# A decoder block on one core: all five engines in an order that the kernel's own clocks set, and a delta-rule chain cut differently

## The chip, the cores and the metric

The kernel runs on one core of one Trainium2 chip. The time is the device time of one execution in microseconds (us). Before: 3033.8 us, the median of three runs (3033.46 to 3036.6).

The core has several engines that run side by side, each with its own queue that it takes in order: TensorE (PE, matrix products, into PSUM), VectorE (DVE), ScalarE (ACT), GpSimd (POOL) and SyncE (SP), which in this kernel issues the DMA transfers. An engine waits where its next instruction needs a result of another engine or of a transfer that isn't there yet.

## The reference

One decoder block over 2048 tokens of width 1024, batch 1, all in 32-bit floats:

```python
mod = einsum(silu(c), ada_w) + ada_b;  shift, scale, gate = split(mod, 3)
h = rmsnorm(x, norm_g) * (1 + scale) + shift
p = h @ w_in                                   # 1024 -> 9344 columns
c_val, c_gate, c_og, ts, r_og, g_conv, g_rwkv = split(p)
y_conv = conv_branch(c_val, c_gate, c_og)      # GLU, depthwise conv of width 31, LayerNorm, swish, SiLU gate, @ w_conv_out
y_rwkv = rwkv7_branch(ts, r_og)                # 16 heads of 64
m = sigmoid(g_conv) * y_conv + sigmoid(g_rwkv) * y_rwkv
x = x + gate * (m @ w_out)
return rmsnorm(x, final_g)
```

The RWKV branch mixes each token's `ts` with that of the token before (token shift), forms r, k, v, a decay w and a rate a per channel, and carries a 64x64 state per head over the tokens:

```python
sk = state @ kk_t
state = state * w_t - sk (x) b_t + v_t (x) k_t
o_t = state @ r_t
```

Then follow a LayerNorm per head, the bonus term sum(r k r_k) v, a SiLU gate and a projection with `w_rwkv_out`.

## The kernel before, in words

**Blocks and groups.** The 2048 tokens are cut into 4 blocks of 512 (b), the 16 heads into 4 groups of 4 (g), and a group into two pairs of heads (q), one pair per 128 partitions. So there are 16 slots (b, g), one after the other in `slot` (L1039), and the state of a group goes on from block to block. All arrays stand with channels on the partitions and 512 tokens along the row.

**Projections.** The columns of `w_in` are 73 tiles of 128. For each tile and block, `project` (L849) makes a 128x512 result in one PSUM bank from 24 matmuls (`mm3k`, L172 to L180; the matmul is L179): eight steps of 128 input channels, and for each the products hi·hi, hi·lo and lo·hi of weights and input that were split into a coarse and a fine part. The weights are split in block 0 (`load_w`, L149 to L170: ACT makes hi, POOL or DVE makes lo), written to DRAM (kh_in, kl_in) and read back in blocks 1 to 3. The input of a block is split by `hprep` (L409) from `hload` (L401). Each slot has 18 projections: k, r and v for its two pairs, two channel tiles of the convolution branch with two projections each, and eight gates. Their filler order is in `FILL` (L46).

**Stages between the projections.** Everything else on PE stands between projection matmuls. A cooperative scheduler (`Task`, `poll`, `tick`, `drain`, L223 to L265) runs while the program is traced: a stage is a piece of a generator that ends in `yield pe, delay`, two constants, the estimated PE time of the stage and a delay until the next one may be placed; `mm3` adds 0.684 us per step of a projection to the clock and polls. On PE the traced order is the order on the chip (`tc.manual_schedule(engines={PE})`, L1084). The order on DVE, ACT, POOL and SP is chosen by the framework's own scheduler, with priorities (`HP`, `LOWP`).

**A pair** (`pair`, L501 to L630): the decay's pre-activation (L513 to L516), its running sum within each chunk of 64 tokens (eight scans of 64 columns on DVE, L522 to L524), its exponentials, the arrays KR and BK (k, r and b scaled by the decay, L544 to L570), the norms of kk (L551), the 128x128 products within each chunk (`As`, L587 with the mask at L590), their strict triangle scaled (`tri`, L597), transposes of BK (`tk`, L607), the bonus (L613), and the values transposed into `uv` (L623).

**A group** (`group`, L645 to L847) takes its two pairs' tiles and goes through these steps:
- The inversion. The 32x32 diagonal blocks of the triangles go to DRAM by 16 small transfers (dA, L657), come back with one block per partition (La, L662), and POOL inverts them in 31 steps of two instructions (L669 to L674). The results go back by way of DRAM (dT, L677, and 16 transfers into As, L684). Two fixed delays of 35 and 25 us stand behind this (L686, L688), and the next stage waits until the group before is done.
- The correction. DVE transposes the blocks (T11, L705); two stages of small matmuls (`lower` L718, `upper` L722, with Qs at L728) make the off-diagonal blocks; no other stage may come between (`locked`).
- The chain: for each of the 8 chunks c, three stages on PE with work on DVE and ACT between them. KR stage (L775): KR times the state S, on 128x128 tiles; DVE adds Xz (L780) and ACT scales the state (Se, L779). Middle stage (L784): the inverse times Xz by head, with the next chunk's `xval` (L749) and the outputs of the chunk before, `olast` (L758), which ACT copies (L762); DVE scales the result into uv (L795). State stage (L800): tk times uv, two matmuls with 128 columns, of which the diagonal 64x64 blocks are used; DVE adds them to Se (S, L804).
- The end: LayerNorm per head (L822 to L831) on DVE, ACT and POOL, a fixed delay of 30 us (L832), transposes back into one PSUM bank `late` (L839), scaling (oc, L841), bonus and gate from DRAM on POOL (L845), and the result to DRAM.

**Beside these**: the convolution (`taps`, L872 to L890: 31 multiply-adds of 128x512 on DVE per channel tile, at low priority), the token shift (`shifted`, L465 to L474, whose first column, L472, and carry, L474, are on DVE), the LayerNorm of the convolution branch of the block before (`lnorm_first`), the norm of the next block's input (`xnorm`), and the splitting of the later weights (`presplit`, L131).

**The second phase** (from L1090): the projections with `w_rwkv_out`, `w_conv_out` and `w_out`, the residual and the final norm.

Of the kernel before, what the change touches and what calls it, by code (L numbers as in the profile page):

```python
# [33 lines left out]
W2 = 4  # L34
# [12 lines left out]
US_MM, US_K = 0.228, 0.684  # L47
LOWP = 1500
# [18 lines left out]
def hybrid_block(ctx: ExitStack, tc: tile.TileContext, x, vecs, convk, w2a2, final_g, ada, w_in, w_co, w_ro, w_o, crow, out,  # L67
                 seq=2048, groups=(0, 1, 2, 3), phase2=True, dbg=None):
    nc = tc.nc
    NB = seq // TB  # L70
    dbg = dbg or {}
# [20 lines left out]
    make_identity(nc, ident)  # L92
# [11 lines left out]

    def rsqrt(y, x_, pool, eng, t=None):
        if t is None:
            t = pool.tile(list(x_.shape), F32, name="rs_t", tag="rs_t")
        eng.tensor_scalar(out=y.bitcast(I32), in0=x_.bitcast(I32), scalar1=-0.5, scalar2=float(0x5F3759DF),
                          op0=ALU.mult, op1=ALU.add)
        for _ in range(3):  # L110
            eng.tensor_tensor(out=t, in0=y, in1=y, op=ALU.mult)
            eng.scalar_tensor_tensor(out=t, in0=t, scalar=-0.5, in1=x_, op0=ALU.mult, op1=ALU.mult)
            eng.scalar_tensor_tensor(out=y, in0=t, scalar=1.5, in1=y, op0=ALU.add, op1=ALU.mult)
# [9 lines left out]
    lo_dve = [False]  # L123
# [7 lines left out]
    def presplit(name, n, half):  # L131

        i = f"{n[0]}_{n[1]}" if name == "o" else n
        back = kept.setdefault((name, n), [dp.tile([P, KT, P], F32R, name=f"k{p_}_{name}{i}", tag=f"k{p_}_{name}{i}")
                                           for p_ in "hl"])
        hs = slice(half * 4, half * 4 + 4)
        st, hi, lo = hx("w_st"), hx("w_hi"), hx("w_lo")
        nc.sync.dma_start(st.rearrange("p (k n) -> p k n", k=4), wsrc[name][n][:, hs, :])
        if name == "o":
            gr = hx("w_gr")  # L140
            nc.sync.dma_start(gr[:, :256], grow_d[n[0] * 256:n[0] * 256 + 256].unsqueeze(0).broadcast_to([P, 256]))
            s4 = st.rearrange("p (k n) -> p k n", n=256)
            nc.gpsimd.tensor_tensor(out=s4, in0=s4, in1=gr[:, :256].unsqueeze(1).broadcast_to([P, 2, 256]), op=ALU.mult)
        nc.scalar.copy(hi.bitcast(F32R), st)
        nc.gpsimd.tensor_tensor(out=lo.bitcast(F32R), in0=st, in1=hi, op=ALU.subtract)
        for d_, s_ in zip(back, (hi, lo)):
            nc.sync.dma_start(d_[:, hs, :].bitcast(F32), s_.rearrange("p (k n) -> p k n", k=4))

    def load_w(name, n, hl=None):  # L149
# [11 lines left out]
        with tc.high_priority(HP):  # L161
            nc.scalar.copy(hi, st)  # L162
            lo_eng = nc.vector if lo_dve[0] or (name != "in" and wcount[0] % 4 < W2) else nc.gpsimd
# [17 lines left out]

    def mm3(ps, w, a):
        for k in range(KT):
            mm3k(ps, w, a, k)
            tick(US_K)
# [35 lines left out]
    now, tasks = [0.0], []  # L221

    class Task:  # L223

        def __init__(self, gen):
            self.gen, self.at, self.cond, self.done = gen, now[0], None, False
            tasks.append(self)

        def ready(self):
            return self.at <= now[0] and (self.cond is None or self.cond())  # L230

        def step(self):
            try:
                r = next(self.gen)
            except StopIteration:
                self.done = True
                tasks.remove(self)
                return
            if callable(r):
                self.cond = r  # L240
            else:
                self.cond = None
                now[0] += r[0]
                self.at = now[0] + r[1]

    def poll():
        moved = True
        while moved:
            moved = False
            for t in list(tasks):  # L250
                if not t.done and t.ready():
                    t.step()
                    moved = True

    def tick(us):
        now[0] += us
        poll()

    def drain(*ts):
        poll()  # L260
        while not all(t.done for t in ts):
            at = [t.at for t in tasks if t.at > now[0] and (t.cond is None or t.cond())]
            assert at, "no task can go on"
            now[0] = min(at)
            poll()  # L265

# [26 lines left out]
    bf = lt.tile([P, P], F32, name="bf", tag="X", bufs=1)  # L293
# [13 lines left out]
    one = c1.tile([P, CH], F32, name="one")  # L307
    nc.vector.memset(one, 1.0)
    maskA = c1.tile([P, 4, CH], F32, name="maskA")
    m64 = lt.tile([64, 2, CH], F32, name="m64", tag="X", bufs=1)  # L310
# [35 lines left out]
    closed = [None]  # L346

    def hx(name):
        return xp.tile([P, TB], F32, name=name, tag="hx")

    def spare(name):
        return closed[0](name) if closed[0] else hx(name)

    def xnorm(b, tts):
        if not tts:
            return
        held = []
        for tt in tts:
            t0 = b * TB + tt * P
            ss = e2.tile([P, 8], F32, name="ss")  # L360
            xh = []
            for half in range(2):
                xt = hx("xt")
                nc.sync.dma_start(xt, x[t0:t0 + P, half * TB:half * TB + TB])
                xh.append(xt)
            for half in range(2):
                nc.scalar.activation(hx("xsq"), xh[half], AF.Square, accum_out=ss[:, half:half + 1])
            vs, rs = ss[:, 2:3], ss[:, 3:4]
            with tc.high_priority(HP):
                nc.vector.tensor_tensor(out=vs, in0=ss[:, 0:1], in1=ss[:, 1:2], op=ALU.add)  # L370
# [668 lines left out]
    def slot(b, g, h, lora, first):  # L1039
        drain(*side, *groups_[-2:-1])  # L1040
        G = opened(b, g, h, lora)
        if first:
            G.wait = 8.0
# [274 lines left out]
```

## Time and profile before

| what | value |
|---|---|
| runs | 3036.6, 3033.8, 3033.46 us |
| median | 3033.8 us |
| the profiled execution | 3034.01 us |
| its span | 3032.2 us |
| granted clock of TensorE, mean | 0.969 |
| DMA | 680.00 MB, 224 GB/s over the span |

The span goes from the first to the last record of the profile; the time of the execution is a little longer. The page gives busy time per engine, groups of instructions by line with the idle time ahead of them and what ended it, and the DMA issues. PE is matrix products, PEld weight loads (they overlap PE), SPq the queue on which SyncE issues transfers; `x` is a count, `tile<-tile` names what is written and what is read, and in a row of the timeline the first two columns are start and duration in us. A record of PE is not always an instruction: a matmul of 32-bit floats leaves two records.

### The profile page before, as it was taken

The page shows a single profiled execution, that of the slowest core. Times are in us where ns is not written, and L with a number is a line of the kernel's source. Part 1 is how long each engine was busy: PE and PEld are TensorE (multiplying, and loading weights), DVE is VectorE, ACT ScalarE, POOL GpSimd, SP SyncE. Part 2 cuts the span into 40 slices and gives each one's busy share as a digit, 9 for nine tenths or more (in the row PEclk, how much of TensorE's full clock was granted, in tenths as well). Part 3 has the DMA queues.
Part 4 walks back from the last instruction along what each step waited for, and adds up shares of the span by engine and source line. Part 5 has one row for each costly group of instructions (what it writes and reads, how often), then busy time and mean ns, then how long its engine had stood idle before and what let it go on. Part 6 is the DMA issues. An engine that isn't in the chain of part 4 may idle for free. (4 is left out here: it accounts for less than half of the span.)

```text
span 3032.2 us, 51026 instructions
## 1 busy us (share of the span) xinstructions
PE 2817.1 (93%) x18640; PEld 2297.6 (76%) x18640; DVE 2072.0 (68%) x4160; ACT 1001.3 (33%) x1936; POOL 1229.8 (41%) x1790
## 2 busy tenths in 40 slices
PE   6889798999799999999999999999999999899998
PEld 5767686777687777777878777778787778788988
DVE  6867777779676778676767777666778755753433
ACT  4424343434233324242423242323323323421211
POOL 3464637352536355425373655253644500400000
PEclk9989899999899999999999999999999999999999
DMA  8677657686757666857676668565656666976665
GB/s 309 234 247 249 217 204 257 204 268 197 241 187 258 198 203 218 284 173 240 191 257 203 210 217 305 168 208 171 193 184 213 237 210 195 336 250 222 215 222 174
DMA packets 363146, 680.00 MB, mean 224 GB/s; under 512 B 135632, under 2 KB 154384, under 8 KB 362896
## 3 DMA queue, kind: packets, MB, share of 16 engines
q1 hardware_dynamic: 362896, 676.75, 67.0%
q8 instruction: 147, 2.41, 0.3%
q14 instruction: 103, 0.84, 0.1%
HBM read 494.08 MB, written 181.41 MB: 223 GB/s over the span
## 5 line engine op out<-in xcount | busy, mean ns | idle before, releaser
L179 PE MATMUL ps_main<-h_hi,w_hi 128*128 128x512 f32 x2304 | 970.6, 421 | 19.7 <-DMA w_hi<-kh_in 15.1
L179 PE MATMUL ps_main<-h_hi,w_lo 128*128 128x512 f32 x2304 | 918.6, 399 | 7.2 <-POOL w_lo L164 4.0
L179 PE MATMUL ps_main<-h_lo,w_hi 128*128 128x512 f32 x2304 | 915.4, 397 | 1.3 <-DVE h_lo L397 1.1
L890 DVE SCALAR_TENSOR_TENSOR acc<-u,ck,acc 128x512 f32<-128x512 f32 x928 | 696.7, 751 | 15.9
L179 PEld LDWEIGHTS ps_main<-h_hi,w_hi 128*128 128x128 f32 x2304 | 442.9, 192 | 115.5 <-issue 9.9
L179 PEld LDWEIGHTS ps_main<-h_hi,w_lo 128*128 128x128 f32 x2304 | 440.7, 191 | 114.4 <-POOL w_lo L164 6.2
L179 PEld LDWEIGHTS ps_main<-h_lo,w_hi 128*128 128x128 f32 x2304 | 443.6, 193 | 81.6 <-DVE h_lo L397 2.9
L804 DVE SCALAR_TENSOR_TENSOR S<-xo,pe,Se 64x64 f32<-64x64 f32 x512 | 144.5, 282 | 140.1 <-PE xo L800 130.5
L671 POOL TENSOR_TENSOR itmp<-La,TT 128x126 f32<-128x126 f32 (+22 forms) x496 | 179.8, 363 | 130.2 <-DMA La<-dA 85.2
L162 ACT CAST w_hi<-w_st 128x1024 fp32r<-128x1024 f32 x103 | 108.1, 1049 | 301.4 <-DMA w_st<-w_co_t 124.8
L673 POOL TENSOR_TENSOR TT<-TT,itmp 128x126 f32<-128x126 f32 (+22 forms) x496 | 191.3, 386 | 36.8
L164 POOL TENSOR_TENSOR w_lo<-w_st,w_hi 128x1024 fp32r<-128x1024 f32 x50 | 120.4, 2408 | 131.2 <-ACT w_hi L162 67.3
L779 ACT ACTIVATE Se<-S,pe 128x128 f32<-128x128 f32 x256 | 88.9, 394 | 169.5 <-DVE S L804 169.4
L164 DVE TENSOR_TENSOR w_lo<-w_st,w_hi 128x1024 fp32r<-128x1024 f32 x53 | 65.6, 1238 | 97.2 <-PE ps_main L179 54.8
L795 DVE TENSOR_TENSOR uv<-xo,rn 64x256 f32<-64x256 f32 x128 | 53.6, 419 | 111.4 <-PE xo L784 99.3
L784 PEld LDWEIGHTS xo<-Xz,As 128*64 128x64 f32 x1024 | 70.0, 138 | 68.8 <-DVE Xz L780 32.0
L753 ACT COPY Xz<-xo 64x256 f32<-64x256 f32 x128 | 47.0, 367 | 211.9 <-PE xo L758 141.7
L780 DVE TENSOR_TENSOR Xz<-xo,Xz 64x256 f32<-64x256 f32 x128 | 53.5, 418 | 86.0 <-PE xo L775 78.9
L845 POOL TENSOR_TENSOR oc<-oc,zt 128x512 f32<-128x512 f32 x64 | 81.7, 1285 | 66.6 <-ACT oc L841 39.6
L784 PE MATMUL xo<-Xz,As 128*64 128x64 f32 x1024 | 87.9, 230 | 20.9 <-DVE Xz L780 20.8
L590 DVE TENSOR_TENSOR As<-aux,maskA 128x512 f32<-128x512 f32 x128 | 83.0, 682 | 30.9 <-PE aux L587 30.4
L587 PE MATMUL aux<-KR,BK 64*128 64x128 f32 x1024 | 82.2, 291 | 17.8 <-DVE As L590 9.3
(299 smaller groups left out, 5493.7 us busy)
## 6 DMA issues: line engine op xcount, KB each, us to landing
w_hi<-kh_in SPq DMA_DIRECT2D x219, 512.0 KB, 4.2
w_lo<-kl_in SPq DMA_DIRECT2D x219, 512.0 KB, 5.3
w_st<-w_in_t SPq DMA_DIRECT2D x73, 512.0 KB, 4.5
kh_in<-w_hi SPq DMA_DIRECT2D x71, 512.0 KB, 2.9
kl_in<-w_lo SPq DMA_DIRECT2D x71, 512.0 KB, 3.6
lny<-y_d SPq DMA_DIRECT2D x72, 256.0 KB, 4.4
w_hi<-kh_ro SPq DMA_DIRECT2D x32, 512.0 KB, 3.9
w_lo<-kl_ro SPq DMA_DIRECT2D x32, 512.0 KB, 5.3
```

The source lines that it names most:

```text
L162: nc.scalar.copy(hi, st)
L164: lo_eng.tensor_tensor(out=lo, in0=st, in1=hi.bitcast(F32), op=ALU.subtract)
L179: nc.tensor.matmul(ps[:, qs], ww[:, k, :], aa[k][:, qs], start=(k == 0 and t == 0 and q == 0), stop=(k == KT - 1 and t == 2 and q == ms - ...
L587: nc.tensor.matmul(pA[hh][:, c // 2, es], BK[hs, cc, es], KR[hs, cc, es], start=(c == 0), stop=(c == 3), skip_group_check=True)
L590: nc.vector.tensor_tensor(out=Asb[:, hh, c4 * 4:c4 * 4 + 4, :].rearrange("p (a e) n -> p a (e n)", e=2), in0=pA[hh], in1=flat(maskA).unsqu ...
L671: nc.gpsimd.tensor_tensor(out=tmp[:, :ni, :nt], in0=La[:, j:j + 1, j + 1:].broadcast_to([P, ni, nt]), in1=TT[:, :ni, j:j + 1].broadcast_to ...
L673: nc.gpsimd.tensor_tensor(out=TT[:, :ni, j + 1:], in0=TT[:, :ni, j + 1:], in1=tmp[:, :ni, :nt], op=ALU.add)
L779: nc.scalar.mul(Se[:, q, :], Sg[:, q, :], R[q]["pe"][:, c:c + 1])
L784: nc.tensor.matmul(b_[pr_, q, hs], As[q][:, hh, c, kcol(e)], Xz[:, e, q, hs], start=(n == 0), stop=(n == 3), skip_group_check=True)
L804: nc.vector.scalar_tensor_tensor(out=Sg[hs, q, hs], in0=b_[hs, 2 + q, hs], scalar=R[q]["pe"][hs, c:c + 1], in1=Se[hs, q, hs], op0=ALU.mult ...
L845: nc.gpsimd.tensor_tensor(out=oc, in0=oc, in1=zt, op=op)
L890: nc.vector.scalar_tensor_tensor(out=acc if i + 1 < HALO else yj, in0=u[:, i:i + TB], scalar=ck[:, j, i:i + 1], in1=acc, op0=ALU.mult, op1 ...
```

## The change

**All engines in traced order.** The handle `nc` is wrapped, so that every instruction is recorded as it is traced, and `manual_schedule()` now holds for all engines. `note` keeps a clock for PE (`now`), DVE, ACT, POOL, SP and the transfers (DMA), and the reckoned end of every tile; a stage yields a condition (`ok` of tiles, `bank` of a PSUM tag, `idle` of an engine, `when` something is done) and is placed when the clocks say that it holds. Constants of time within the tasks (35, 25 and 30 us among them) fall away.

```diff
+    def note(name, op, out, ins):
+        t = max([now[0], vt.get(name, 0.0), used.get(k_, 0.0)] + [ready.get(key(a), 0.0) + SEM for a in ins])
...
+        if name == "PE":
...
+                c = 0.015 + N_ / 2400 if kd == F32R else 2 * max(0.107 * M_ / 128, N_ / 1200) * (
+                    0.55 if K_ <= 64 else 0.75 if M_ <= 64 else 1.0)
+            if kd != kind[0]:
+                kind[0], c = kd, c + SWITCH
...
+        elif name == "SP":
+            vt["SP"] = t + 0.07
+            vt["DMA"] = max(vt["DMA"], t) + size(out) * out.shape[0] * 4 / DMA_RATE
+            end = vt["DMA"] + 1.9
+        else:
+            c0, c1_ = RATE[name]
+            end = vt[name] = t + c0 + c1_ * max([size(out)] + [size(a) for a in ins[:1]])
...
-    with tc.manual_schedule(engines={mybir.EngineType.PE}):
+    with tc.manual_schedule():
```

Weights come through a class `Load`, two projections ahead (three where they come back from DRAM); rings of buffers (`hx`, `t2`, `w`) give a buffer out when it is free; the steps after a projection (token shift, gates, convolution input) are tasks of their own (`evac`). The DVE taps are placed when DVE's clock is at most 0.7 us ahead. The next block's input is split within the last projection of a block (`khook`). The last slot has its own filler order (`LAST`). Block 0's projections with `w_rwkv_out` and `w_conv_out`, the first of the second phase, are traced by the tasks too while the last group ends (`early_rows`). Side work (LayerNorm of the convolution branch, `presplit`, `xnorm`) runs as one task of low rank, with `lnorm_first` in group 2 and the presplits 2, 2, 0, 4 per slot instead of 2 in each.

**The pair.** ACT adds 1, and one scan over 512 columns, with a multiplier `keep` that is 0 at the start of each chunk, takes the place of eight:

```diff
-        for c in range(NCH):
-            cs = slice(c * CH, c * CH + CH)
-            nc.vector.tensor_tensor_scan(out=M[:, cs], data0=one, data1=M[:, cs], initial=0.0, op0=ALU.add, op1=ALU.add)
...
+        nc.scalar.activation(M, M, AF.Identity, bias=one1[:, 0:1])
+        yield ok(M)
+        nc.vector.tensor_tensor_scan(out=M, data0=keep, data1=M, initial=0.0, op0=ALU.mult, op1=ALU.add)
```

In `shifted` the first column and the carry move to ACT:

```diff
+        nc.scalar.activation(dst[:, 0:1], ps[:, 0:1], AF.Identity, scale=mu1[:, mi:mi + 1], bias=carry[:, mi:mi + 1])
+        nc.scalar.activation(carry[:, mi:mi + 1], ps[:, TB - 1:TB], AF.Identity, scale=mu)
...
-        nc.vector.scalar_tensor_tensor(out=dst[:, 0:1], in0=carry[:, mi:mi + 1], scalar=mu, in1=t1[:, 0:1],
-                                       op0=ALU.mult, op1=ALU.add)
-        lastv[0] = nc.vector.tensor_copy(carry[:, mi:mi + 1], ps[:, TB - 1:TB])
```

**The inversion.** The 16 dA transfers and both La loads are issued when both pairs' triangles are reckoned to be done; each POOL step waits until POOL's clock is at most 0.5 us ahead; the As transfers go in fours; the correction waits for the chain of the group before, not for its end:

```diff
-        yield lambda: G.tri == 2
+        yield when(lambda: G.tri == 2)
+        yield ok(*As)
...
+        yield ok(La, TT)
         for j in range(31):
+            yield idle("POOL", 0.5)
...
+        yield ok(dT)
...
-        yield 0.0, 35.0
...
-        yield 0.0, 25.0
-        yield lambda: G.pairs == 2 and (before is None or before.done)
+                yield idle("SP", 0.1)
+        yield when(lambda: G.pairs == 2 and (before is None or before.chained))
+        yield ok(*As)
```

**The chain.** The outputs leave the middle stage and become a stage of their own after each odd chunk, for two chunks whose matmuls come by turns on the two halves of the array's columns; the state stage works by head, with four products of 64x64 by turns on the halves, in place of two of 128x128:

```diff
         def olast(c):
-            vr, rc = vrow(c % 2), rcol(c % 2)
             for n, (q, hh, hs) in enumerate(every):
-                nc.tensor.matmul(xo[c % 2][vr, q, hs], As[q][:, hh, c, rc], uv[:, c, q, hs],
-                                 start=False, stop=(n == 3), skip_group_check=True)
+                for e in range(2):
+                    nc.tensor.matmul(xo[e][vrow(e), q, hs], As[q][:, hh, c + e, rcol(e)], uv[:, c + e, q, hs],
+                                     start=False, stop=(n == 3), skip_group_check=True)
+            with tc.high_priority(HP):
+                for e in range(2):
+                    nc.scalar.copy(O[vrow(e), c // 2], xo[e][vrow(e), 0:2])
...
-            if c:
-                olast(c - 1)
...
-            yield 1.1, 2.5
-            for q in range(2):
-                nc.tensor.matmul(b_[:, 2 + q, :], R[q]["tk"][:, c, :], uv[:, c, q, :], start=False, stop=(q == 1),
-                                 skip_group_check=True)
+            yield ok(uv)
+            for q, hh, hs in every:
+                nc.tensor.matmul(b_[hs, 2 + q, 0:64], R[q]["tk"][:, c, hs], uv[:, c, q, hs], start=False,
+                                 stop=(q + hh == 2), skip_group_check=True)
...
-            yield 0.6, 3.3
-        olast(NCH - 1)
-        ocopy(NCH - 1)
+            yield ok(Sg)
+            if e:
+                olast(c - 1)
+                yield ok(uv)
+        G.chained = True
```

**The end of a group.** Bonus and gate are loaded ahead of the transposes, which wait for the reckoned end of the norm and for the bank instead of 30 us.

More of the change, by code (lines that the diff above doesn't have):

```diff
@@ L33 @@
 HP = 3000
-W2 = 4
+W2 = 0.3
 HB = 8
@@ new lines, in until, with drain, after, ok @@
+    def until(pred):
+        poll()
+        while not pred():
+            ws = [w for w in (t.when() for t in tasks) if w is not None and w > now[0]]
+            assert ws, "no task can go on"
+            now[0] = min(ws)
+            poll()
+    def drain(*ts):
+        until(lambda: all(t.done for t in ts))
+    def after(us):
+        at = now[0] + us
+        return lambda: at
+    def ok(*aps):
+        ks = [key(a) for a in aps]
+        return lambda: max(ready[q] for q in ks)
+    def idle(name, us):
+        return lambda: vt[name] - us
@@ L919, in lnorm_first @@
+        yield both(ok(ys), free, bank("late"))
         ps = pl.tile([P, TB], F32, name="late", tag="late")
```

856 lines of the change are left out of this document (565 added, 291 removed).

## The prediction

> **What bounds the kernel now.** I read the page first, then the busy times by stretch, then the waits of TensorE alone, and last the timeline of single stages.
>
> ```profile
> span 3032.2 us, 51026 instructions
> PE 2817.1 (93%) x18640; PEld 2297.6 (76%) x18640; DVE 2072.0 (68%) x4160; ACT 1001.3 (33%) x1936; POOL 1229.8 (41%) x1790
> ...
> 56.00:2440.00 2384.00, 2222.04 (x15052) 1782.09 (x15050) 1747.47 (x3529) 825.92 (x1581) 1166.81 (x1736) 0.97 0.67 221
> 2440.00:3032.20 592.20, 565.22 (x3467) 492.67 (x3467) 281.44 (x514) 150.13 (x312) 44.25 (x29) 0.98 0.68 229
> ```
>
> TensorE (PE) is busy 93% of the span, and no other engine comes near. In the two lines by stretch the columns are the stretch, then busy time of PE, weight loads, VectorE (DVE), ScalarE (ACT) and GpSimd (POOL), then clock and DMA. The first stretch is the part that the change rewrites; in it PE idles 2384.0 - 2222.0 = 162 us. The second is mostly code that the change leaves alone. So there are two ways to gain: fewer idle microseconds out of 162, or less PE work. What ends the idle time, in the first stretch (us in total, times, longest):
>
> ```profile
> PE late L839 <- POOL uv L831: 23.3, 4, 16.1
> PE xo L784 <- DVE Xz L780: 20.8, 14, 3.8
> PE ps_main L179 <- DMA w_hi<-kh_in: 15.1, 3, 5.8
> PE late L839 <- ACT oc L841: 14.4, 15, 1.1
> PE aux L587 <- DVE As L590: 9.3, 7, 4.5
> PE late L722 <- DVE Qs L728: 9.1, 8, 1.9
> PE late L718 <- DVE T L705: 7.9, 2, 4.6
> PE aux L587 <- POOL KR L570: 7.8, 6, 2.8
> PE xo L758 <- DVE S L804: 7.5, 3, 4.4
> ```
>
> These rows hold 115 us; the other 47 lie in rows under 6 us each. PE takes its instructions in the order in which the program is traced, so each row is a stage that was traced too early for its data.
>
> **The change, part by part: PE work.** A short stage interrupts the projection matmuls. Those follow each other at 54.70/240 = 0.228 us (row below). I price a stage as the start of the second projection matmul after it, less the start of the last one before it, less two times 0.228.
>
> ```profile
> 2651.57 54.70 PE ps_main L179 x240
> ```
> ```profile
> 546.89 0.40 PE L179 MATMUL ps_main<-h_hi,w_lo 128*128 128x512 f32 x1
> ...
> 547.73 0.63 PE L758 MATMUL xo<-uv,As 128*64 128x64 f32 x8
> ...
> 548.63 0.40 PE L179 MATMUL ps_main<-h_lo,w_hi 128*128 128x512 f32 x1
> ...
> 550.93 0.39 PE L179 MATMUL ps_main<-h_hi,w_lo 128*128 128x512 f32 x1
> 551.16 0.60 PE L800 MATMUL xo<-uv,tk 128*128 128x128 f32 x4
> ...
> 551.83 0.40 PE L179 MATMUL ps_main<-h_lo,w_hi 128*128 128x512 f32 x1
> ```
> ```profile
> 523.48 0.40 PE L179 MATMUL ps_main<-h_hi,w_lo 128*128 128x512 f32 x1
> 523.81 0.27 PE L784 MATMUL xo<-Xz,As 128*64 128x64 f32 x1
> ...
> 524.27 0.22 PE L749 MATMUL xo<-uv,As 128*64 128x64 f32 x1
> ...
> 524.77 0.40 PE L179 MATMUL ps_main<-h_lo,w_hi 128*128 128x512 f32 x1
> ```
> ```profile
> 517.30 0.40 PE L179 MATMUL ps_main<-h_hi,w_lo 128*128 128x512 f32 x1
> 517.63 0.63 PE L551 MATMUL aux<-bones,sq 128*64 128x2 f32 x16
> ...
> 518.53 0.40 PE L179 MATMUL ps_main<-h_lo,w_hi 128*128 128x512 f32 x1
> 518.77 0.40 PE L179 MATMUL ps_main<-h_hi,w_lo 128*128 128x512 f32 x1
> 519.09 0.68 PE L749 MATMUL xo<-uv,As 128*64 128x64 f32 x8
> ...
> 520.04 0.40 PE L179 MATMUL ps_main<-h_lo,w_hi 128*128 128x512 f32 x1
> ```
>
> Per chunk now: the middle stage with its outputs costs 548.63 - 546.89 - 0.456 = 1.28, the same stage in a first chunk, without outputs, 524.77 - 523.48 - 0.456 = 0.83, and the state stage 551.83 - 550.93 - 0.456 = 0.44. So outputs that ride along cost 0.45. The last fence shows why turns look good and what they cost. L749 alone, eight records (a matmul of f32 leaves two) on one half of the columns, costs 520.04 - 518.77 - 0.456 = 0.81. L551, sixteen records that alternate between the halves, within one PSUM tile, costs 518.53 - 517.30 - 0.456 = 0.77. Turns halve the time of a record. But a stage on 128x64 tiles has a fixed part: from 523.81 to 524.27 fifteen records follow at 0.031, sixteen are 0.49, and 0.83 - 0.49 = 0.34 remains. A stage on the whole array, 0.44 for four records, shows none: its second row follows its first at projection pace.
>
> After the change the outputs of two chunks (sixteen records in turns) are a stage of their own, 0.83 per two chunks, and the state stage becomes eight records in turns on 128x64: 0.83 less eight records at 0.031, 0.58 (no row has just this; not below 0.25, the records alone, nor above 0.81, L749 without overlap; I take 0.58 because L551 overlaps within one tile). Two chunks cost 2 x (1.28 + 0.44) = 3.44 before and 2 x (0.83 + 0.58) + 0.83 = 3.65 after. There are 128 chunks: 64 x 0.21 = **+13 us**, with ends 64 x 2 x (0.25 - 0.58) = -42 and 64 x 2 x (0.81 - 0.58) = +29 around that. So the part that saves matmul time pays it back in tile changes. In the built programs' order such changes of tile size number 555 before and 895 after.
>
> The Trainium skill says as much: "TensorEngine Tiling (Array Packing)", section "Key Properties", has a change of tiling mode, as against a change of tile, drain TensorE; the 0.34 above agrees. Its section "Theoretical Speedup" gives up to twice the rate for a small dimension of 64 or less: by that alone outputs and state stage would halve, 128 x (0.45 + 0.44) / 2, an estimate of 57 us gained.
>
> **Waits that go.** In the changed program a stage is placed by readiness and by a free PSUM bank, not by a constant. Between the last state stage and the final transposes (L839) its order has 63 to 144 projection matmuls, 14 to 33 us, and the second transpose waits for its bank behind more of them: of 37.7 us I keep 5, -33. Chain (20.8 + 7.5): the steps now have only 3 to 9 projection matmuls between them, 0.7 to 2.1 us, where DVE may still be inside a tap; I keep a third, -19. The correction stage (9.1 + 7.9): -14. The block boundary (15.1): the next input is now split inside the last projection; I keep 5, -10. The pair stages (17.1): kept, since their DVE and POOL work is the same. Of the 47 in small rows: -20. Together **-96**, between 0 and -150.
>
> **Moved: the inversion's round trip.** The changed program issues all sixteen small dA transfers of a group in one run on SP after the second pair's tiles; both La loads follow, and the POOL steps stand on POOL's queue from the time its clock gives.
>
> ```profile
> 2009.66 6.60 SPq L684 DMA_DIRECT2D As<-dT  x14
> ```
> ```profile
> 2095.32 1.13 SPq L662 DMA_DIRECT2D La<-dA  x2
> ```
> ```profile
> L673 POOL TENSOR_TENSOR TT<-TT,itmp 128x126 f32<-128x126 f32 (+22 forms) x496 | 191.3, 386 | 36.8
> L671 POOL TENSOR_TENSOR itmp<-La,TT 128x126 f32<-128x126 f32 (+22 forms) x496 | 179.8, 363 | 130.2 <-DMA La<-dA 85.2 <-DMA w_lo<-kl_in 9.6
> ```
> ```profile
> La<-dA SPq DMA_DIRECT2D x32, 256.0 KB, 4.5
> ...
> As<-dT SPq DMA_DIRECT2D x256, 16.0 KB, 1.9
> ...
> dT<-TT SPq DMA_DIRECT2D x32, 128.0 KB, 4.0
> ```
> ```profile
> L705 DVE STREAM_TRANSPOSE T<-As 32x128 f32<-32x128 f32 x128 | 31.0, 277 | 9.5 <-DMA As<-dT 8.2
> ```
>
> One small transfer holds SP for 6.60/14 = 0.47 us, where the new clock (SP's line in note) reckons 0.07. A group needs: sixteen issues 7.5, La 0.6 and its landing 4.5, POOL (191.3 + 179.8)/16 = 23.2, dT 0.5 + 4.0, sixteen issues back 7.5, landing 1.9, eight transposes 2.2: 52 us, plus what else POOL does in between, 3 us or more. What PE has to do meanwhile is in the order: in the last group of each block 153 to 171 projection matmuls stand between the second pair's tiles and the inversion's first matmul, 35 to 39 us, 40 to 47 with the other stages among them; in the other twelve groups 237 to 318, 54 to 73 us, 66 to 86 with the stages (before: 216 to 279 everywhere). So four groups come out short, by 11, 11, 8 and 15 us: **+45** (0 if other waits of PE cover it). While POOL stands at the first step, the next pair's KR and BK queue behind it, and PE's L587 behind those; while SP stands at the As transfers, weight loads queue behind it, and they are issued two projections ahead (2 x 24 x 0.228 = 11 us), which covers a 7.5 us run and a landing of about 4 just so.
>
> **Off the path.** 256 scans of 64 columns become 32 masked scans of 512:
>
> ```profile
> L524 DVE TENSOR_TENSOR_SCAN M<-one,M 128x64 f32<-128x64 f32 x256 | 90.9, 420 | 8.4 <-ACT M L516 8.1
> ```
>
> A long scan costs between one short one and eight (0.42 to 3.4 us); DVE saves up to 78 us and loses at most 18. The token shift's first column and the carry move from DVE to ACT. Neither engine bounds: DVE is busy 1747 of 2384. I cost this at nothing; if DVE were the cover that is gone, the scan alone is worth -78 to +18. The chunk after an output stage now waits for two ACT copies of the outputs; a chain has 96 to 117 projection matmuls (22 to 27 us) where it had 249 to 297, in a slot of some 2384/16 = 149 us, so its length costs nothing.
>
> **Sum.** The profiled execution took 3034.0 us for its span of 3032.2, and the median of the runs is 3033.8. 3034 + 13 - 96 + 45 = **2996 us**, 1.2% faster.
>
> **Rivals.** (1) *All waits go and the four inversions are covered*: the in-order queues fit, PE idles a tenth of the 162: 3034 + 13 - 130 = 2917. For it: all the idle time above is misplacement. Against: SP's 0.47 against 0.07. (2) *Slower: the inversion comes late in every group.* With every engine in a fixed order, POOL's steps are stretched by what stands among them and waits itself; the 52 us grow. From 14 us of such stretching on, the twelve other groups (66 us and more) fall short as well; at 24 us each they lose 10: 12 x 10 + 4 x 10 more on the last groups = 160. With 60 of the waits gone: 3034 + 13 - 60 + 45 + 160 = 3192 at the full price, 3080 at a third of it. For it: POOL waited 85.2 us for La already. Against: PE's own waits shift everything with them. (3) *Waits only change places*: what goes, 96, comes back as the inversions' 45 and about 38 at the pair stages and correction stages, because DVE and POOL are as late as now: 3034 + 13 - 96 + 45 + 38 = 3034, within 6 us of the median. (4) *It doesn't do what it says*: the state stage's turns don't overlap: 0.81 instead of 0.58, 2996 + 29 = 3025, and less wait gone with it: about 3032.
>
> **How the numbers follow.** Forecast 0.42 (2960 to 3027); rival 1 0.20; rival 2 0.26; rival 3 0.08; rival 4 0.04. This kernel's runs tell 0.2%, 6 us, from no change. Faster: 0.42 + 0.20 = 0.62; same: 0.12; slower: 0.26. The range leaves out the far end of rival 1 and the upper half of rival 2: 2905 to 3105; the likeliest case alone has 2960 to 3027.
>
> **What would show it.** In the new profile all lines fall on one helper, so go by tiles. Right: the state stage xo<-uv,tk is 128x64 and a lone stage of it costs 0.5 to 0.65 us; PE's waits at late<-T,As are some 10 us in the groups that end a block and small elsewhere; waits at late<-ident,uv nearly gone. Wrong: PE idle over 162 in the first part; waits at late<-T,As in all sixteen groups (rival 2); a state stage at 0.8 (rival 4) or near 0.3 (then the turns pay); DVE without idle time.

## The result, and the profile after

The changed kernel takes 3041.7 us (median of 20 runs, 3030.7 to 3056.6), the kernel before 3033.6 us beside it (20 runs, 3025.3 to 3039.9). The ratio is 1.0032 with a 95% interval of 1.0022 to 1.0043: 8 us slower, where 2996 and a gain of 1.2% were forecast. The profiled execution of the changed kernel took 3035.0 us, at the low end of its runs, so the profile explains what became of the forecast gain, and only part of the 8 us.

The head of the page and the two stretches of the prediction, in the changed kernel (stretch, then busy time of PE, weight loads, DVE, ACT and POOL, then clock and DMA):

```profile
span 3033.3 us, 51847 instructions
PE 2803.0 (92%) x19152; PEld 2222.4 (73%) x19152; DVE 2074.1 (68%) x3738; ACT 1064.6 (35%) x2168; POOL 1269.0 (42%) x1790
```
```profile
56.00:2440.00 2384.00, 2220.58 (x15587) 1721.60 (x15585) 1753.82 (x3122) 892.83 (x1815) 1194.63 (x1739) 0.97 0.67 222
2440.00:3033.30 593.30, 554.49 (x3434) 480.01 (x3434) 278.29 (x500) 146.63 (x308) 60.92 (x35) 0.97 0.67 224
```

In the first stretch PE idled 162 us before; now it is 2384.0 - 2220.6 = 163 us. In the second it idled 592.2 - 565.2 = 27 us, and now 593.3 - 554.5 = 39. The idle time that the prediction counted on has not gone. What ends it, in the whole profile (us in total, times, longest):

```profile
PE late L126 <- DVE T L126: 48.7, 9, 17.1
PE ps_main L126 <- ACT w_hi L126: 21.9, 7, 6.9
...
PE aux L126 <- POOL KR L126: 14.6, 14, 3.5
PE ps_main L126 <- ACT o_hi L126: 13.9, 1, 13.9
PE ps_main L126 <- DMA w_hi<-kh_in: 12.2, 6, 3.6
PE xo L126 <- ACT Xz L126: 11.0, 16, 2.5
PE ps_main L126 <- ACT h_hi L126: 7.6, 2, 5.9
PE late L126 <- POOL uv L126: 7.1, 6, 2.9
...
PE aux L126 <- DVE As L126: 5.6, 5, 1.6
...
PE late L126 <- DVE Qs L126: 3.1, 2, 1.6
...
PE xo L126 <- DVE Xz L126: 2.4, 7, 0.5
```

Three rows of the kernel before that the prediction doesn't show, for comparison:

```profile
PE ps_main L179 <- ACT w_hi L162: 4.3, 1, 4.3
...
PE xo L775 <- ACT Xz L753: 2.7, 2, 2.4
...
PE ps_main L179 <- ACT o_hi L1100: 1.4, 1, 1.4
```

Set beside the rows of before, the rows are new almost throughout. The final transposes waited 23.3 us for uv and now 7.1, the chain 20.8 for Xz on DVE and now 2.4, the correction 9.1 for Qs and now 3.1. In their place PE waits 48.7 us at the correction for the inverted blocks (10.8 before: 7.9 at L718 into late and 2.9 into aux), 21.9 for weights that ACT splits in block 0 (4.3), 14.6 for KR (7.8), 13.9 at the start of the second phase (1.4), 11.0 for Xz on ACT (2.7) and 7.6 for the next block's input.

The longest of these waits, in group 3 of block 1. First SP's queue, with the sixteen transfers out (dA) at 1179.81 and the sixteen back (As) from 1234.98, then PE, then four stretches around it:

```profile
1179.37 0.38 SPq L126 DMA_DIRECT2D w_lo<-kl_in  x1
1179.81 9.20 SPq L126 DMA_DIRECT2D dA<-As  x16
1190.33 1.12 SPq L126 DMA_DIRECT2D La<-dA  x2
...
1195.69 0.43 SPq L126 DMA_DIRECT2D w_hi<-kh_in  x1
```
```profile
1230.91 1.35 SPq L126 DMA_DIRECT2D dT<-TT  x2
1234.98 1.75 SPq L126 DMA_DIRECT2D As<-dT  x4
1236.83 0.38 SPq L126 DMA_DIRECT2D u_d<-lny  x1
1237.24 5.67 SPq L126 DMA_DIRECT2D As<-dT  x12
```
```profile
1201.42 0.77 PE L126 MATMUL ps_main<-h_hi,w_hi 128*128 128x512 f32 x1 [3.54 <-DMA w_hi<-kh_in]
...
1227.06 0.40 PE L126 MATMUL ps_main<-h_hi,w_lo 128*128 128x512 f32 x1
1244.59 0.23 PE L126 MATMUL late<-T,As 32*32 32x32 f32 x1 [17.13 <-DVE T L126]
```
```profile
1210.00:1227.00 17.00, 16.45 (x70) 12.72 (x70) 12.74 (x17) 5.75 (x10) 14.93 (x28) 1.00 0.92 328
1227.00:1244.00 17.00, 0.46 (x2) 0.03 (x1) 6.76 (x15) 5.16 (x9) 5.82 (x12) 0.60 0.48 125
1244.00:1252.00 8.00, 7.41 (x138) 6.00 (x139) 1.84 (x6) 1.23 (x2) 2.71 (x3) 0.56 0.36 98
1252.00:1260.00 8.00, 7.54 (x57) 5.55 (x58) 3.55 (x11) 3.02 (x7) 0.00 (x0) 1.00 0.12 33
```

Three things are to be seen. PE runs out of projections at 1227.5, while the inverted blocks only start back at 1235 and take until 1242.9 to be issued: 5.67/12 = 0.47 us each, as before. Between 1179.8 and 1195.7 no weight load gets onto SP's queue: first come the sixteen transfers, then the two La loads and some stores and loads; at 1201.4 PE has stood 3.5 us for the load of 1195.7. The four waits over 1.5 us for w_hi from DRAM all come this way, behind a run of dA: these loads were issued 5.7 to 7.5 us ahead of the matmul that uses them, where the median over all loads of w_hi from DRAM is 14.8 us. And after the 17 us wait the granted clock is 0.56 for 8 us: part of the wait is paid a second time. The Trainium skill, "TensorE: Matmul & The Clock Gate", section "HAM oscillation — how this bites in real kernels", says that an idle gap of more than about 3.4 us halves TensorE's clock. The long wait agrees: the clock stands at 0.50 from 1230.5, 3.1 us into the wait, to 1251.0, 6.4 us behind it. But six waits of 1.6 to 2.6 us in this run are followed by 3.4 us at 0.50 as well (1.74 us up to 2037.6, then 0.50 from 2039.5 to 2042.9), and others of up to 2.9 us are not.

### The profile page after: what moved, and what is told of

Read it like the earlier page. It is cut to its first block, busy times and chain, and to the rows that moved or that the text cites. A ratio compares the mean times of both kernels' runs of the same rounds, so it can differ in the third digit from the quotient of the medians.

```text
span 3033.3 us, 51847 instructions
## 1 busy us (share of the span) xinstructions
PE 2803.0 (92%) x19152; PEld 2222.4 (73%) x19152; DVE 2074.1 (68%) x3738; ACT 1064.6 (35%) x2168; POOL 1269.0 (42%) x1790
## 4 chain that ended last, share of the span: by engine, by line
PE 48%; POOL 15%; DVE 15%; DMA 10%; issue 5%; SPq 4%; ACT 2%; POOLq 0%; DVEq 0%; ACTq 0%
PE ps_main L126 32%; PE xo L126 7%; POOL TT L126 5%; POOL itmp L126 5%; PE pout L126 4%; SPq L126 4%; DVE acc L126 4%; PE aux L126 3%; DMA La<-dA 1%; DVE As L126 1%; PE late L126 1%; POOL lny L126 1%; DVE gst L126 1%; POOL uv L126 1%; DMA As<-dT 1%
## 5 line engine op out<-in xcount | busy, mean ns | idle before, releaser
L126 PE MATMUL ps_main<-h_hi,w_hi 128*128 128x512 f32 x2304 | 980.5, 426 | 44.1 <-ACT w_hi L126 21.9
L126 POOL TENSOR_TENSOR w_lo<-w_st,w_hi 128x1024 fp32r<-128x1024 f32 (+1 forms) x82 | 164.2, 2002 | 312.6 <-ACT w_hi L126 297.3
L126 POOL TENSOR_TENSOR itmp<-La,TT 128x126 f32<-128x126 f32 (+22 forms) x496 | 195.6, 394 | 131.9 <-DMA La<-dA 101.1
L126 POOL TENSOR_TENSOR TT<-TT,itmp 128x126 f32<-128x126 f32 (+22 forms) x496 | 213.0, 430 | 38.9
L126 ACT CAST w_hi<-w_st 128x1024 fp32r<-128x1024 f32 (+1 forms) x135 | 127.3, 943 | 278.2 <-DMA w_st<-w_co_t 126.3
L126 ACT ACTIVATE th<-ps_main 128x512 f32<-128x512 f32 x160 | 95.4, 596 | 346.8 <-PE ps_main L126 273.6
L126 POOL TENSOR_TENSOR lny<-lny 128x512 f32<-128x512 f32 x90 | 118.2, 1321 | 108.5 <-DMA lny<-y_d 83.6
L126 PE MATMUL xo<-uv,As 128*64 128x64 f32 x2048 | 133.0, 229 | 1.4 <-DVE As L126 0.8
L126 PEld LDWEIGHTS xo<-uv,As 128*64 128x64 f32 x2048 | 106.2, 138 | 28.2 <-issue 24.4
L126 DVE TENSOR_TENSOR w_lo<-w_st,w_hi 128x1024 fp32r<-128x1024 f32 x53 | 74.0, 1396 | 73.6 <-PE ps_main L126 51.9
L126 ACT ACTIVATE Se<-S,pe 128x128 f32<-128x128 f32 x256 | 88.7, 394 | 80.8 <-DVE S L126 79.8
```

The costliest lines, as they stand in the source:

```text
L126: r = f(*a, **k)
```

## The experiments

Each was timed beside the kernel before on the same chip; ratios are to that. A difference to the changed kernel is one of medians from different sets of runs, in which the kernel before took 3029.4 to 3033.6 us, so a few us of it mean nothing. "Order held" means that the clocks are fed what the changed kernel's own instructions would have fed them, so that every engine takes its instructions in the changed kernel's order, and only the edited work differs; in the traces of `state_fixed`, `half_issues`, `double_issues` and `state_half` DVE, ACT and POOL indeed take the changed kernel's instructions in its order.

**Theory A**: the clocks reckon an issue on SP at 0.07 us where it holds SP for 0.47, so the correction comes too early in PE's order. **Rival B**: the waits only change places. **Rival C**: the fixed order on DVE, ACT, POOL and SP is the harm. **Theory D**: the state stage in turns costs PE time.

### Undo one thing, order free

`state_old`, the state stage on 128x128 again:

```diff
-            for q, hh, hs in every:
-                nc.tensor.matmul(b_[hs, 2 + q, 0:64], R[q]["tk"][:, c, hs], uv[:, c, q, hs], start=False,
-                                 stop=(q + hh == 2), skip_group_check=True)
+            for q in range(2):
+                nc.tensor.matmul(b_[:, 2 + q, :], R[q]["tk"][:, c, :], uv[:, c, q, :], start=False, stop=(q == 1),
+                                 skip_group_check=True)
...
```

> The changed kernel with the state stage as before: two matmuls of 128x128 instead of four of 64x64 by turns. Stage work (theory): a lone state stage costs 0.585 us in turns and 0.449 on the whole array, so 128 x 0.136 = 17 us go, 3042 to about 3025. Rival (the chain's stages hide in waits that PE has anyway, so what goes at the stage comes back as idle time): 3042, no change beyond 4 us.

Measured: 3055.4 us, 1.0085 (1.0064 to 1.0106): slower than the changed kernel, by 14 us of the medians and 16 by the ratios, not faster.

`late10`:

```diff
         yield ok(*As)
+        yield after(10.0)
```

> The changed kernel with one delay of 10 us on the clock ahead of the correction stage, so that DVE's block transposes, the correction and the whole chain of a group are traced 10 us later; nothing else. Theory A (the clocks reckon the inversion's round trip 8 to 13 us short, and that alone makes TensorE stand at the correction for 48.7 us in nine groups): these waits fall below 10 us, and the time by 30 to 40, to about 3007. Rival B (the waits only change places, because DVE, POOL and the transfers behind them are what is late): the waits at the correction fall, others grow by as much, 3042 within 8.

Measured: 3102.4 us, 1.0240 (1.0223 to 1.0256). The waits at the correction fell from 48.7 to 11.2 us, but others grew by more:

```profile
PE late L126 <- POOL uv L126: 26.7, 6, 14.3
PE ps_main L126 <- ACT h_hi L126: 21.2, 5, 9.7
...
PE ps_main L126 <- DMA w_hi<-kh_in: 16.0, 9, 3.2
...
PE late L126 <- DVE T L126: 11.2, 3, 7.3
```

`sp_true`:

```diff
-            vt["SP"] = t + 0.07
+            vt["SP"] = t + 0.45
```

> The changed kernel with one figure of its clocks changed: an issue on SP is reckoned at 0.45 us instead of 0.07, which is what the trace shows. Theory A: the sixteen issues to and from DRAM around the inversion are then reckoned at 7 us each way, the correction comes about 12 us later in the order, and the time falls by 30 to 40, to about 3007. Rival B (waits change places): 3042 within 8. Rival C (SP's queue itself is the trouble, since later issues put weight loads later in the order): slower than 3050.

Measured: 3053.6 us, 1.0068 (1.0048 to 1.0087). The waits at the correction fell to 27.2 us, and PE then waited 29.1 us for o_hi and 22.1 us for w_lo on POOL. So theory A's remedy, a clock that reckons the issue right, does not help while the issues themselves stay: 12 us slower than the changed kernel, in a new order.

`pe_only`:

```diff
-    with tc.manual_schedule():
+    with tc.manual_schedule(engines={mybir.EngineType.PE}):
```

> The changed kernel, but only TensorE keeps the traced order; the order on the other four engines is left to the framework's scheduler, as before the change. Rival C (the fixed order on DVE, ACT, POOL and SP makes the new waits: a store or a load stands behind one that waits): 3042 falls by 25 or more, since 57 us of new waits at weights, inputs and pair stages go. Theory A (the order on TensorE is the trouble): within 15 us of 3042, with the waits at the correction still there. If the fixed order on the other engines is a gain: slower than 3060.

Measured: 3239.7 us, 1.0690 (1.0671 to 1.0710):

```profile
PE late L126 <- DVE T L126: 95.7, 9, 19.8
PE xo L126 <- DVE Xz L126: 38.7, 42, 3.3
```

Rival C falls: with this order on PE, the order that the clocks write on the other engines is worth 198 us against the one that the scheduler makes with the priorities that are left. The first three runs look like rival B: whatever moves an order moves the waits. They don't say whether the waits could go without a new order. For that the order has to be held.

### Change the work, order held

`state_fixed`: the edit of `state_old`, and the clock reckons the two matmuls as it did the four.

```diff
+                if key(ins[0]).startswith("tk"):
+                    c = 4 * max(0.107 / 2, 64 / 1200) * 0.75
```

> The state stage on 128x128 again, two matmuls, but the clock reckons it as it does the four 64x64 ones, so every engine keeps exactly the changed kernel's order; only TensorE's work differs. Theory D (work decides when the order is held; the 16 us more of the earlier run were the rearranged order): 128 x (0.585 - 0.449) = 17 us less than the changed kernel's 3042, about 3025, with waits within 10 us of the changed kernel's. Rival B (a stage's work hides in waits): 3042 within 5.

Measured: 3041.8 us, 1.0037 (1.0021 to 1.0053): as the changed kernel, with runs from 3027 to 3054. So what `state_old` lost goes with its new order and not with the stage's work. The 17 us of theory D do not show.

`half_issues`: the two heads of a transfer go together, eight issues of 32 KB each way in place of sixteen of 16 KB.

```diff
-                    for hh in range(2):
-                        nc.sync.dma_start(dA[q, hh, :, e, bk].rearrange("c s t -> s c t"), As[q][sl, hh, e::2, sl])
+                    tc.nc.sync.dma_start(dA[q, :, :, e, bk].rearrange("h c s t -> s h c t"), As[q][sl, :, e::2, sl])
+                    for hh in range(2):
+                        note("SP", "dma_start", dA[q, hh, :, e, bk], [As[q][sl, hh, e::2, sl]])
...
-                    for hh in range(2):
-                        nc.sync.dma_start(As[q][sl, hh, e::2, sl], dT[:, q, hh, :, e, bk, :])
+                    tc.nc.sync.dma_start(As[q][sl, :, e::2, sl], dT[:, q, :, :, e, bk, :])
+                    for hh in range(2):
+                        note("SP", "dma_start", As[q][sl, hh, e::2, sl], [dT[:, q, hh, :, e, bk, :]])
```

> The changed kernel, order of all engines held, but the sixteen small transfers each way around an inversion are issued as eight that carry both heads. At 0.47 us of SP each, the round trip shortens by about 3.8 us each way, 7.5 in all. Theory A with the order held: the nine waits at the correction (17.1, 9.2, 5.9, 4.3, 4.1, 3.3 and three smaller, 48.7 in all) shrink by 7.5 each, to about 12 in all, and the time falls by 37 and by part of the half-clock stretches behind them, to about 3000. Rival B (what TensorE gains there it waits for elsewhere, since DVE, POOL and the transfers are late all the same): falls by less than 12, to 3030 or more.

Measured: **2966.5 us**, 0.9770 (0.9746 to 0.9794), 75 us less than the changed kernel (79 by the ratios), where theory A expected some 40. Its page and its waits:

```profile
span 2965.7 us, 51597 instructions
PE 2786.8 (94%) x19152; PEld 2218.4 (75%) x19152; DVE 2076.7 (70%) x3738; ACT 1065.3 (36%) x2168; POOL 1265.4 (43%) x1790
```
```profile
PE late L126 <- DVE T L126: 28.3, 7, 13.9
...
PE ps_main L126 <- ACT o_hi L126: 14.3, 1, 14.3
PE ps_main L126 <- ACT w_hi L126: 12.2, 4, 4.9
PE ps_main L126 <- DVE w_lo L126: 11.5, 8, 4.8
...
PE ps_main L126 <- DMA w_hi<-kh_in: 2.1, 1, 2.1
...
PE late L126 <- POOL uv L126: 1.8, 3, 0.7
```

The correction gives 48.7 - 28.3 = 20 us, not 37: the longest wait falls from 17.1 to 13.9 us, not by 7.5. But the weights give 10 + 10 us (w_hi from DRAM and from ACT), uv 5 and KR 5, while the wait for w_lo on DVE grows by 5 and the one at o_hi stays. PE's idle time (span less busy time) falls from 230 to 179 us. The granted clock rises from 0.968 to 0.975, and PE's busy time falls by 16 us.

`double_issues`: each of the sixteen is cut in two.

```diff
...
+                        for n in range(2):
+                            tc.nc.sync.dma_start(As[q][sl, hh, e + 4 * n:e + 4 * n + 3:2, sl],
+                                                 dT[:, q, hh, 2 * n:2 * n + 2, e, bk, :])
```

> The changed kernel, order of all engines held, but each of the sixteen small transfers each way around an inversion is cut in two: 32 issues, some 15 us of SP each way in place of 7.5. Theory A: every inversion comes 15 us later than in the changed kernel; all sixteen corrections wait, 16 x 12 and more, and the half-clock stretches come on top: 3042 to 3200 or more. Rival (SP has room, and the gain of the merged kernel came from the transfers' own time, which cutting hardly changes): under 3080.

Measured: 3279.0 us, 1.0811 (1.0794 to 1.0827). The waits, and the transfers themselves in the changed kernel and in this one (duration on SP's queue in ns, least, median and most):

```profile
PE late L126 <- DVE T L126: 126.5, 14, 23.7
PE ps_main L126 <- DMA w_hi<-kh_in: 67.2, 9, 11.9
PE ps_main L126 <- ACT w_hi L126: 48.2, 6, 14.3
```
```profile
L126 SPq DMA_DIRECT2D As<-dT x256: 302/430/1154, 196.7 to 2443.8; - x128
```
```profile
L902 SPq DMA_DIRECT2D As<-dT x512: 302/425/1588, 203.8 to 2692.2; - x171
```

An issue of half the bytes holds SP just as long, so SP is held twice as long in all: by the medians from start to start within a run (0.474, 0.470 and 0.494 us), 243 us over the kernel with sixteen, 481 with 32, 126 with eight. The time goes +237 us for 238 more, and -75 for 117 less. The transfers themselves land sooner when they are smaller (1.7 us against 2.0 for As, and 3.4 for the merged ones), so it isn't their own time. Two rows go with it most: w_hi from DRAM with 12.2, 67.2 and 2.1 us at 16, 32 and 8 issues, and the correction with 48.7, 126.5 and 28.3.

`state_half`, the edits of `state_fixed` and `half_issues` together, with nothing else:

```diff
-            for q, hh, hs in every:
+            for q in range(2):
...
+                    tc.nc.sync.dma_start(dA[q, :, :, e, bk].rearrange("h c s t -> s h c t"), As[q][sl, :, e::2, sl])
...
```

> Both of the above together, order held. If both effects are real and add up: 3042 - 17 - 40 = about 2985, faster than the kernel before. Rival B: about 3025.

Measured: 2958.1 us, 0.9756 (0.9743 to 0.9770). The state stage adds 8 us by the medians and 4 by the ratios, with intervals that overlap: whether it adds anything is not shown.

`state_quarter`, both pairs' transfers merged as well (one buffer for the tiles of both), four each way. The edit also lays the loads of the modulation two to a buffer, and 28 of DVE's 3738 instructions, near the start, stand in another order:

```diff
+                    if q == 0:
+                        tc.nc.sync.dma_start(dA[:, :, :, e, bk].rearrange("q h c s t -> s (q h) c t"), G.A4[sl, :, e::2, sl])
...
+                    if q == 0:
+                        tc.nc.sync.dma_start(G.A4[sl, :, e::2, sl], dT[:, :, :, :, e, bk, :].rearrange("s q h c t -> s (q h) c t"))
```

> The changed kernel, order held, state stage on 128x128, and the transfers of both pairs merged as well: four each way in place of sixteen (the tiles of a group's two pairs lie in one buffer). Against the run with eight, 2958, SP is held 1.9 us less each way. If the price per issue stays (75 us for 256 issues less, 0.29 each), 128 less give 37: 2921. If the waits that an inversion causes are mostly gone by then (28 us left at the correction, one of 14), less than 12: 2946 or more.

Measured: **2947.3 us**, 0.9721 (0.9706 to 0.9736), faster than the kernel before by 85 us and than the changed one by 94. It gives 11 us for 128 issues less, where the step from sixteen to eight gave 75 for 256: little of what SP's runs cost seems to be left. The 13.8 us wait of group 3 in block 1 and the 13.9 us at o_hi are still there.

### One part alone in the kernel before

`b_state`, with the four matmuls by turns in the state stage:

```diff
-            for q in range(2):
-                nc.tensor.matmul(b_[:, 2 + q, :], R[q]["tk"][:, c, :], uv[:, c, q, :], start=False, stop=(q == 1),
+            for q, hh, hs in every:
+                nc.tensor.matmul(b_[hs, 2 + q, 0:64], R[q]["tk"][:, c, hs], uv[:, c, q, hs], start=False,
...
```

> The kernel before with one part of the change: the state stage by head, four matmuls of 64x64 by turns. Its place in TensorE's order comes from constants and stays. By the stage's measured price it gets 128 x 0.136 = 17 us slower, 3033 to 3050; if turns were the gain that they look like, it is faster; if the stage hides in waits, within 5 us.

Measured: 3035.0 us, 1.0016 (1.0006 to 1.0026): 5 us slower. Here and in `b_half` only PE's order is held.

`b_chain`, with the outputs of two chunks as a stage of their own as well, placed by constants of the kernel's kind:

```diff
-            yield 0.6, 3.3
-        olast(NCH - 1)
-        ocopy(NCH - 1)
+            yield 0.6, 3.3
+            if e:
+                olast(c - 1)
+                yield 0.8, 1.8
...
```

> The kernel before with the chain of the changed one: state stage by head in turns, and outputs of two chunks as a stage of their own after each odd chunk, placed by constants. The prediction's term: +13 us, 3044. From the run of the state stage alone, +5, and outputs at 0.82 per two chunks in place of 2 x 0.45, -5: about 3031, no change.

Measured: 3052.3 us, 1.0067 (1.0053 to 1.0081): 20 us slower. Its waits for uv at the final transposes are 36.5 us (23.3 before) and for Qs 17.0 (9.1); PE's busy time is 2817.4 us, and 2817.1 in the kernel before. So what the profiled execution loses in its span, 16 us, is waits and not PE work; that they come from the longer chain under constants that were fitted to the other is likely but not shown.

`b_half`, with the merged transfers:

```diff
...
+                    nc.sync.dma_start(dA[q, :, :, e, bk].rearrange("h c s t -> s h c t"), As[q][sl, :, e::2, sl])
...
+                    nc.sync.dma_start(As[q][sl, :, e::2, sl], dT[:, q, :, :, e, bk, :])
```

> The kernel before, with only the small transfers around each inversion merged, eight each way in place of sixteen. If an issue on SP has its price in any order, the kernel before gains what the changed one gained, about 75 us, to 2957. If the changed kernel is sensitive to it because its order was set by clocks that reckon 0.07 us for an issue (theory A), the kernel before, whose correction stages wait 10.8 us in all, gains at most 20: 3010 to 3031.

Measured: 2993.2 us, 0.9869 (0.9852 to 0.9886): 40 us faster, between the two expectations. The kernel before pays for SP's runs too, but half as much; the scheduler's order on the other engines changed with the edit, so what the issues alone are worth here is less sure. Its three waits for w_hi from DRAM, 15.1 us, become one of 2.7.

```profile
span 2989.9 us, 50756 instructions
PE 2801.4 (94%) x18640; PEld 2289.5 (77%) x18640; DVE 2074.7 (69%) x4160; ACT 998.3 (33%) x1936; POOL 1224.2 (41%) x1790
```

## Why the prediction was wrong

**PE work, +13: the price of a lone stage right, its effect in the time not borne out.** The state stage in the changed kernel, ahead of and behind it the projection matmuls:

```profile
1263.13 0.39 PE L126 MATMUL ps_main<-h_hi,w_lo 128*128 128x512 f32 x1
1263.45 0.45 PE L126 MATMUL xo<-uv,tk 128*64 128x64 f32 x8
1263.84 0.50 PE L126 MATMUL ps_main<-h_hi,w_hi 128*128 128x512 f32 x1
1264.17 0.40 PE L126 MATMUL ps_main<-h_lo,w_hi 128*128 128x512 f32 x1
```

1264.17 - 1263.13 - 0.456 = 0.58 us, the value taken. As forecast, the stage got dearer (0.44 before) although its records are busy 58.1 us in all instead of 79.8. By that price the state stage alone is 128 x 0.14 = 18 us. The runs show less: 5 us in the kernel before, nothing in `state_fixed`, 4 to 8 in `state_half`. And PE's busy time did not grow by 13 us with the change: it went from 2817.1 to 2803.0.

**Waits that go, -96: this is the step that failed, in the small rows and in what it left as covered.** At the transposes, the chain and Qs of the correction the waits went about as forecast. At the block boundary 3 us went, not 10. But of the 47 us in small rows 20 were to go, and no new row was priced. Instead six rows grew by 57 us: w_hi on ACT 17.6, o_hi 12.5, Xz on ACT 8.3, h_hi 7.6, KR 6.8, w_lo on DVE 4.1. So PE's idle time stayed at 163 us in the first stretch, where the forecast took 51 away (96 less 45).

With them fell the sentence that weight loads behind a run of As transfers are covered, two projections ahead, "just so" (7.5 us and a landing of 4 are more than the 11 that it sets against them; and the order has three projections ahead for weights from DRAM). In the four longer waits it was not the run of As but that of dA, which the sentence leaves out, with what stands behind it: 13.7 to 16.3 us pass from one weight load on SP to the next. SP's queue was counted only as a leg of the inversion's round trip, and everything behind a run waits for it too. With half of the issues and the order held, the kernel gained 75 us; with twice as many it lost 237.

That does not account for every new row. In `half_issues` 40 of the 57 us are still there (o_hi 12.9, w_lo on DVE 9.5, w_hi on ACT 7.9, Xz on ACT 4.6, h_hi 4.0, KR 1.4). What causes these is open.

**The inversion, +45: close in size, not in its parts.** The waits at the correction grew by 38 us; the four groups that end a block have 4.3, 17.1, 5.9 and 9.2 of the 48.7. Nine groups wait, though, not four. From the first dA to the last issue of As it takes 61 to 92 us, where the sum has 48 and "3 us or more". POOL's steps are stretched by what stands among them: 32.5 to 60.6 us for 22.8 to 29.3 us of their own work, most in group 2 of block 2. That so long a trip costs no more than forecast is luck; PE's other waits, which let it come later too, are a likely reason, not shown.

**The clock was not priced at all.** A wait of 17 us brings 8 us at 0.56. But the clock does not explain the miss, since its mean is 0.969 before and 0.968 after; it adds to what the other runs gain and lose. Over the runs the mean granted clock goes with the idle time: 0.977 in `state_quarter` (span less busy time 172 us), 0.968 in the changed kernel (230), 0.949 in `pe_only` (376), 0.933 in `double_issues` (424).

**The rival that came nearest** is the third, "waits only change places". It describes what happened, but its reason (DVE and POOL as late as now) is not the one that the runs show. (The first rival's 2917 is a slip: a tenth of 162 us left idle means 146 gone, not 130, and 2901.)

**Was the idea wrong?** With sixteen issues the change costs 0.3%. With eight, the changed kernel is at 0.977 and the one before at 0.987 of the kernel before, so the change gains 1%. The step to eight is thus worth 35 to 40 us more to the changed kernel than to the one before, most of the 46 us by which the forecast missed (38 of gain, 8 of loss). That 1% is near the forecast's 1.2% is luck, however: between these two runs PE's idle time falls by 10 us (188.5 to 178.9), where the forecast had 51, and its busy time by 15 (2801.4 to 2786.8), where it had 13 more. Why the busy time falls is not shown.

What stays open: what holds the 40 us of new waits that half of the issues leave, why the changed kernel's own runs spread over 26 us, why `state_fixed` shows nothing of the state stage's time, and why `late10` loses 60 us when its waits at the correction all but go. In the last one other waits and the clock make up the sum, but no run separates their causes.

## What to carry to other kernels

When the order is fixed on every engine, price each queue as a resource and count what stands behind a run of small transfers, not only what the run is for; halving the number of the small transfers was worth 75 us here in one kernel and 40 in the other. To test a theory about waits, hold the order and change only the work: the runs in which the order was free only showed that waits move. And price a long wait of TensorE at more than its length, since the matmuls behind it can run at half the clock for some us (6.4 us behind the wait of 17.1).

## What the runs showed of the hardware that was not expected

An issue takes 0.43 to 0.45 us of SP's queue (0.47 to 0.49 from start to start) whether it carries 8, 16 or 32 KB; with 64 KB it takes 0.48 out and 0.62 back. The granted clock falls to half around every wait of TensorE over 3 us (20.5 us at 0.50 for the wait of 17.1), except for the one at the start, and behind six of those between 1.6 and 2.6 us (3.4 us at 0.50 each). And one masked scan over 512 columns, 1.33 us, is cheaper than eight of 64, which took 90.9 us for 256, 2.84 for eight:

```profile
L126 DVE TENSOR_TENSOR_SCAN M<-keep,M 128x512 f32<-128x512 f32 x32 | 42.6, 1330 | 15.0 <-ACT M L126 14.8
```

DVE saves 48 us, within the bounds given, and, as DVE doesn't bound, no run shows it in the time.
